# Second halves of the stacked keys, copied by transfers within SBUF

## The chip, the cores and the metric

The kernel runs on one core of one Trainium2 chip. The metric is the device time of one execution in microseconds (us). The core's engines work side by side, each down a list of its own in order: TensorE (PE, matrix products; its weight loads are listed as PEld), VectorE (DVE), ScalarE (ACT), GpSimd (POOL) and SyncE (SP), which here does nothing but issue transfers. An engine waits where an instruction needs a result of another one, and semaphores carry that.

## The reference, cut to what matters

One transformer block on a sequence of 512 rows of width 1024, in fp32: a modulation of `c` (`ada`), a layer norm, projections, two kinds of attention, an output projection, and a feed-forward part with a causal convolution.

```
mod = silu(c) @ w_ada + b_ada
u = layer_norm(x) * (1 + sc1) + sh1
qa, ka, va, qb, kc, vc, ksl, vsl, kw, vw, gl = split(u @ w_in)
o_a = dilated_attention(rope(qa), rope(ka), va)           # 8 heads of 64
o_b = nsa_attention(rope(qb), rope(kc), vc, rope(ksl), vsl, rope(kw), vw, gl, ...)
y = concat([o_a, o_b]) @ w_o
x = layer_norm(ALPHA * x + g1 * y, ln1_g, ln1_b)
u = layer_norm(x) * (1 + sc2) + sh2
a_gate, a_val = split(u @ w_up)
h = gelu(causal_dwconv(a_gate, conv_w, conv_b)) * a_val
x = layer_norm(ALPHA * x + g2 * (h @ w_down), ln2_g, ln2_b)
```

What the change touches are the scores, a query times the keys of a head (64 numbers each), for the dilated attention (`ka`) and for two of the three branches of the other (`ksl`, `kw`).

## The kernel before

Products are made at fp32 accuracy from fp32r operands: each operand is split into a high part (the value copied by ACT into fp32r, which rounds it) and a low part (the value less the high part, by DVE), and three products high x high, low x high and high x low are added up (`mm3`, the lines 259 to 261).

For scores this is done with a stack. A head has 64 rows, PE takes 128. `q_stack` puts the high part of a query in one half of the 128 partitions and its low part in the other half: `qe` for the head in the lower half, `qo` for the one in the upper half. `k_half` makes two tiles of 128 x 512 for a head: `hh` (named khh) with the key's high part in both halves, and `ll` (kll) with its low part in both halves. One product of the query stack with khh then gives high x high + low x high, and a second with kll adds the rest (lines 700 and 701). `e` says in which half of the transposed keys (`pt`, named qT) the head stands: `b` is its own half, `c0` the other one.

`k_half` runs 12 times: four times for the other attention's keys in the opening (`kb`, through `k_stack`, lines 1270 and 1273; khh_853/kll_854, 859/860, 910/911, 916/917) and twice for each of the four quads of dilated heads, a0 to a3 (line 955).

Time runs in stages. Up to about 55 us the modulation, the layer norm and the first products run; to 300 us the attention. There, PE's products of the remaining projections (`quad`, weights 512 KB each, loaded by SP into four buffers `wraw`, split by ACT and DVE into whi and wlo) fill the room between the rows of attention. A row of attention is a chain over the engines: scores on PE (L700, L701), mask and minimum on DVE (L708, `sa_`), exponential on ACT (L714), reciprocal on DVE (L719), scaling on POOL (L722), transposes on PE (L727), a split on ACT and DVE (L746, L750), products with the values on PE (L775). Compressed keys have a chain of their own (L645 to L675, with `pc` and `sm_`). Beside these stand the columns of the modulation (`ada_col`: a load and one DVE product with a sum, L1019) and its rows (`ada_row`, `arow`), and the two-layer compression (`hid`, with the weights k_w1 and v_w1). The output projection w_o, the up projection (325 to 540 us) and the down projection (to the end) follow.

All loads of weights go through `load` (L240) on SP's queue, one behind the other in the list: an entry that waits holds those behind it. Each transfer there also waits for the one eight places ahead of it in the list to have landed, as the kernel is built.

The order of the instructions on each engine is not that of the program text alone: the code interleaves generators (`fill_one`, `run_misc`), and the scheduler of the tile framework places each instruction by a simulated time at which its operands are ready. So a change in `k_half` also changes the order elsewhere.

Of the kernel before, what the change touches and what calls it, by code (L numbers as in the profile page):

```python
# [14 lines left out]
AF = mybir.ActivationFunctionType  # L15
# [91 lines left out]
def body(ctx, tc, nc, a, out, dbg=None):  # L107
# [59 lines left out]
    V, A, P, T = nc.vector, nc.scalar, nc.gpsimd, nc.tensor  # L167
# [68 lines left out]
    def f(x):  # L236
        return x.bitcast(F32)

    def load(dst, src, queue=nc.sync):
        queue.dma_start(dst, src)  # L240
# [230 lines left out]
        V.tensor_sub(o[0:64], pt[64:128], f(o[64:128]))  # L471
        return e, o

    def k_half(pt, e, mk=t2):
        b, c0 = 64 * e, 64 - 64 * e
        hh, ll = mk('khh'), mk('kll')
        A.activation(hh[b:b + 64], pt[b:b + 64], AF.Copy)
        A.activation(hh[c0:c0 + 64], pt[b:b + 64], AF.Copy)
        V.tensor_sub(ll[b:b + 64], pt[b:b + 64], f(hh[b:b + 64]))
        V.tensor_copy(ll[c0:c0 + 64], f(ll[b:b + 64]))  # L480
        return hh, ll

    def k_stack(pt, mk=t2):
        return [k_half(pt, e, mk) for e in range(2)]
# [446 lines left out]
    def a_post(j):  # L931
        mk = to if j == 0 else t2

        def run(banks):
            ys = []
            for b in range(2):
                yield from wk_wait(1)
                ys.append(evac_half(banks[b], b, 2, P))
                acc_done()
                yield 1 + b * PD  # L940
            yield from acc_wait()
            live[0] += 1
            pt = transposed(ys, 0, 'acc')
            yield 2
            qa[j] = q_stack(pt, mk)
            acc_done()
            yield 3
            yield from acc_wait()
            live[0] += 1
            pt = transposed(ys, 1, 'acc')  # L950
            wlive[0] -= 2
            yield 2
            ka[j] = []
            for b in range(2):
                ka[j].append(k_half(pt, b, mk))
                if b == 1:
                    acc_done()
                    ready.add(('a', j))
                yield
        return run  # L960
# [585 lines left out]
```

## Time and profile before

| | us |
|---|---|
| median of 3 runs | 726.68 |
| lowest and highest | 724.72, 728.5 |
| profiled execution | 726.39 |
| its span, from the first to the last instruction | 724.6 |

In the span, PE is busy 95%, DVE 64%, ACT 48%, POOL 34%. Busy time is a sum over stages of different kinds; what bounds a stage is read from the stretch itself: from the instruction before which PE stood idle, and from what released it. The granted clock of PE is given as a share of full speed, 1.00 being its upper level (2.4 GHz) and 0.50 its lower (1.2 GHz).

### The profile page before, as it was taken

The page shows a single profiled execution, that of the slowest core. Times are in us where ns is not written, and L with a number is a line of the kernel's source. Part 1 is how long each engine was busy: PE and PEld are TensorE (multiplying, and loading weights), DVE is VectorE, ACT ScalarE, POOL GpSimd, SP SyncE. Part 2 cuts the span into 40 slices and gives each one's busy share as a digit, 9 for nine tenths or more (in the row PEclk, how much of TensorE's full clock was granted, in tenths as well). Part 3 has the DMA queues.
Part 4 walks back from the last instruction along what each step waited for, and adds up shares of the span by engine and source line. Part 5 has one row for each costly group of instructions (what it writes and reads, how often), then busy time and mean ns, then how long its engine had stood idle before and what let it go on. Part 6 is the DMA issues. An engine that isn't in the chain of part 4 may idle for free.

```text
span 724.6 us, 10875 instructions
## 1 busy us (share of the span) xinstructions
PE 691.1 (95%) x3964; PEld 596.8 (82%) x3964; DVE 464.8 (64%) x961; ACT 345.7 (48%) x697; POOL 248.7 (34%) x273
## 2 busy tenths in 40 slices
PE   7999899999889998999999999999999999999995
PEld 6999788987879887778898888888888788888884
DVE  7879966766986889988843344464443364544236
ACT  5647665752767689916553333333333341222101
POOL 2002436441277475511310110111111355666216
PEclk9999999999999999999999999999999999999998
DMA  9955342046451011260112224434423233343002
GB/s 340 386 207 206 131 135 86 30 174 238 140 204 60 29 60 58 86 235 1 59 60 87 88 88 145 140 135 161 145 88 116 88 107 126 116 146 121 25 15 101
DMA packets 29149, 89.93 MB, mean 124 GB/s; under 512 B 3748, under 2 KB 4516, under 8 KB 29096
## 3 DMA queue, kind: packets, MB, share of 16 engines
q1 hardware_dynamic: 28660, 89.05, 35.6%
q8 instruction: 31, 0.51, 0.3%
q10 hardware_dynamic: 436, 0.18, 0.1%
q14 instruction: 22, 0.18, 0.1%
HBM read 87.13 MB, written 2.10 MB: 123 GB/s over the span
## 4 chain that ended last, share of the span: by engine, by line
PE 51%; DVE 3%; POOL 1%; issue 1%; ACT 0%; POOLq 0%; DVEq 0%
PE d L261 6%; PE d L260 6%; PE d L259 5%; PE pvv L259 5%; PE pvv L261 5%; PE pvv L260 5%; PE pg L259 5%; PE pg L261 5%; PE pg L260 5%; DVE x L1355 1%; PE wo L261 1%; PE wo L260 1%; PE wo L259 1%; DVE x L1346 0%; DVE bn L299 0%
## 5 line engine op out<-in xcount | busy, mean ns | idle before, releaser
L256 DVE TENSOR_TENSOR wlo<-wraw,whi 128x1024 fp32r<-128x1024 f32 x60 | 86.2, 1437 | 124.8 <-ACT whi L255 123.6
L255 ACT ACTIVATE whi<-wraw 128x1024 fp32r<-128x1024 f32 x60 | 63.6, 1060 | 142.9 <-PE pg L260 70.4
L259 PE MATMUL quad<-whi,u 128*128 128x256 f32 x256 | 75.0, 294 | 1.0 <-DVE qo L471 1.0
L260 PE MATMUL quad<-wlo,u 128*128 128x256 f32 x256 | 72.8, 284 | 0.0
L261 PE MATMUL quad<-whi,u 128*128 128x256 f32 x256 | 72.6, 284 | 0.0
L1498 POOL TENSOR_TENSOR wraw<-wraw,arow 128x1024 f32<-128x1024 f32 x22 | 57.8, 2633 | 35.3 <-DMA wraw<-w_down 28.6
L259 PE MATMUL pg<-u,whi 128*128 128x512 f32 (+1 forms) x176 | 67.7, 385 | 0.0
L260 PE MATMUL pg<-u,whi 128*128 128x512 f32 (+1 forms) x176 | 66.8, 380 | 0.0
L261 PE MATMUL pg<-u,wlo 128*128 128x512 f32 (+1 forms) x176 | 66.8, 379 | 0.0
L261 PE MATMUL pvv<-u,wlo 128*128 128x512 f32 (+1 forms) x176 | 66.8, 379 | 0.0
L259 PE MATMUL pvv<-u,whi 128*128 128x512 f32 (+1 forms) x176 | 66.8, 379 | 0.0
L260 PE MATMUL pvv<-u,whi 128*128 128x512 f32 (+1 forms) x176 | 66.8, 379 | 0.0
L256 POOL TENSOR_TENSOR hl<-cv,hh 128x512 fp32r<-128x512 f32 x14 | 23.9, 1705 | 110.8 <-ACT hh L255 110.8
L259 PEld LDWEIGHTS quad<-whi,u 128*128 128x128 f32 x256 | 48.7, 191 | 5.7 <-issue 3.9
L708 DVE CUSTOM_DVE_ANT_0 p<-sp,masks 128x128 f32<-128x128 f32 (+1 forms) x96 | 45.0, 482 | 8.8 <-PE sp L701 7.9
L260 PEld LDWEIGHTS quad<-wlo,u 128*128 128x128 f32 x256 | 48.9, 191 | 1.0 <-issue 0.4
L261 PEld LDWEIGHTS quad<-whi,u 128*128 128x128 f32 x256 | 48.9, 191 | 0.1
L727 PE MATMUL pT<-ident,p 128*128 128x128 f32 x240 | 39.8, 280 | 4.6 <-POOL p L722 4.2
L260 PEld LDWEIGHTS pg<-u,whi 128*128 128x128 f32 x176 | 33.1, 188 | 6.6 <-issue 0.5
L256 POOL TENSOR_TENSOR hg<-cv,hg 128x512 fp32r<-128x512 f32 x8 | 12.9, 1609 | 74.9 <-ACT hg L255 74.9
L259 PEld LDWEIGHTS pg<-u,whi 128*128 128x128 f32 x176 | 33.1, 188 | 6.6 <-issue 0.5
L261 PEld LDWEIGHTS pvv<-u,wlo 128*128 128x128 f32 x176 | 33.1, 188 | 6.3
(636 smaller groups left out, 1884.7 us busy)
## 6 DMA issues: line engine op xcount, KB each, us to landing
wraw<-w_up SPq DMA_DIRECT2D x44, 512.0 KB, 3.2
wraw<-w_down SPq DMA_DIRECT2D x22, 512.0 KB, 3.4
ada<-ada_col SPq DMA_DIRECT2D x32, 256.0 KB, 6.0
wraw<-w_quad SPq DMA_DIRECT2D x16, 512.0 KB, 4.9
wraw<-ada_col SPq DMA_DIRECT2D x16, 512.0 KB, 3.3
wraw<-ada_row SPq DMA_DIRECT2D x16, 512.0 KB, 3.6
x<-x SPq DMA_DIRECT2D x8, 512.0 KB, 4.8
wraw<-w_o SPq DMA_DIRECT2D x8, 512.0 KB, 3.2
```

Of the source, the lines that this page charges most:

```text
L255: A.activation(hi, raw, AF.Copy)
L256: lo_engine.tensor_sub(lo, raw, f(hi))
L259: T.matmul(o_, sh, mh, start=start, stop=False)
L260: T.matmul(o_, sh, ml, start=False, stop=False)
L261: T.matmul(o_, sl, mh, start=False, stop=stop)
L708: V.tensor_tensor_reduce(p[:, cols[i]], e['s'][:, cols[i]], masks[:, m0:mask0 + 512], 1.0, 3e38, op0=ALU.add, op1=ALU.min, accum_out=m_[:, ...
L727: T.transpose(e['t'][:, 128 * j:128 * j + 128], e['p'][:, 128 * j:128 * j + 128], ident)
L1355: V.scalar_tensor_tensor(src[:, hs], src[:, hs], ag[:, 3:4], b_[h][:, cs], op0=ALU.mult, op1=ALU.add)
L1498: P.tensor_mul(w, w, g2)
```

## The change

In `k_half` the second copy of the high part (an ACT copy into the other half) and of the low part (a DVE copy into the other half) are replaced by two transfers from SBUF to SBUF of 64 x 512 fp32 (128 KB), on SP's queue. A new argument `spare` is true by default, and no call sets it, so all 12 calls take the new way; the four lines of the old way stay in the text behind it, unused.

```diff
-    def k_half(pt, e, mk=t2):
+    def k_half(pt, e, mk=t2, spare=True):
         b, c0 = 64 * e, 64 - 64 * e
+        if spare:
+            hh, ll = mk('khh'), mk('kll')
+            A.activation(hh[b:b + 64], pt[b:b + 64], AF.Copy)
+            load(f(hh[c0:c0 + 64]), f(hh[b:b + 64]))
+            V.tensor_sub(ll[b:b + 64], pt[b:b + 64], f(hh[b:b + 64]))
+            load(f(ll[c0:c0 + 64]), f(ll[b:b + 64]))
+            return hh, ll
         hh, ll = mk('khh'), mk('kll')
         A.activation(hh[b:b + 64], pt[b:b + 64], AF.Copy)
         A.activation(hh[c0:c0 + 64], pt[b:b + 64], AF.Copy)
```

Line numbers behind this place rise by 7: the mask step of the softmax is L708 before and L715 now.

The order of DVE in the opening, before. `kll_911` and `kll_917` are the low parts of the second pair of keys, `qe_927` and `qo_928` the second query stack, `wraw_1002` a column load of the modulation, `p_981` the first row's softmax.

```order
L479 TENSOR_TENSOR kll_911<-qT_905,khh_910 64x512
L1019 ISA wraw_1002,mod_164<-wraw_1002,crow_86,b_col_78 128x1024
L1019 ISA mod_164 128x1
L480 CAST kll_911<-kll_911 64x512
L479 TENSOR_TENSOR kll_917<-qT_905,khh_916 64x512
L708 ISA p_981,sa__982<-sp_969,masks_709 128x128
L708 ISA sa__982 128x1
L480 CAST kll_917<-kll_917 64x512
L708 ISA p_981,sa__982<-sp_969,masks_709 128x256
L708 ISA sa__982 128x1
L470 TENSOR_TENSOR qe_927<-qT_922,qe_927 64x512
L471 TENSOR_TENSOR qo_928<-qT_922,qo_928 64x512
```

And the same place now:

```order
L480 TENSOR_TENSOR kll_911<-qT_905,khh_910 64x512
L1026 ISA wraw_975,mod_164<-wraw_975,crow_86,b_col_78 128x1024
L1026 ISA mod_164 128x1
L480 TENSOR_TENSOR kll_917<-qT_905,khh_916 64x512
L470 TENSOR_TENSOR qe_927<-qT_922,qe_927 64x512
L471 TENSOR_TENSOR qo_928<-qT_922,qo_928 64x512
L715 ISA p_981,sa__982<-sp_969,masks_709 128x128
L715 ISA sa__982 128x1
L715 ISA p_981,sa__982<-sp_969,masks_709 128x256
L715 ISA sa__982 128x1
```

The two copies are gone, the query stack comes ahead of the softmax, and the product with the column load stands here with `wraw_975`, which before stood ahead of the first query stack; the one with `wraw_1002` is now 12 rows behind this piece, after two more softmax steps. On PE the score products of the second and third group stand 13 and 12 places further ahead than before; the first product of a1's first row with kll stands 18 places further back.

The order of SP at the same time, as a piece of the difference (a row with + is new):

```order
 L240 DMA wraw_975<-ada_col 128x1024
+L240 DMA khh_853<-khh_853 64x512
+L240 DMA kll_854<-kll_854 64x512
+L240 DMA khh_859<-khh_859 64x512
+L240 DMA kll_860<-kll_860 64x512
+L240 DMA khh_910<-khh_910 64x512
 L240 DMA wraw_989<-w_quad 128x1024
+L240 DMA kll_911<-kll_911 64x512
+L240 DMA khh_916<-khh_916 64x512
+L240 DMA kll_917<-kll_917 64x512
 L240 DMA wraw_1002<-ada_col 128x1024
 L240 DMA wraw_1030<-ada_col 128x1024
```

The eight transfers of the opening stand between four weight loads; the load of k_w1 follows the last row shown.

The order of DVE at a2 (about 250 us), before. `pc` and `sm_` belong to two rows of the compressed keys' chain, `pcl` to the row ahead of them.

```order
L479 TENSOR_TENSOR kll_3233<-qT_3215,khh_3232 64x512
L646 TENSOR_TENSOR pc_3266<-pc_3266,sc_3206 128x256
L480 CAST kll_3233<-kll_3233 64x512
L647 TENSOR_REDUCE sm__3265<-pc_3266 128x8
L655 TENSOR_REDUCE sm__3221<-pc_3222 128x8
L479 TENSOR_TENSOR kll_3250<-qT_3215,khh_3249 64x512
L648 TENSOR_TENSOR pc_3266<-pc_3266,sm__3265 128x256
L480 CAST kll_3250<-kll_3250 64x512
L656 RECIPROCAL sm__3221<-sm__3221 128x8
L675 TENSOR_TENSOR pcl_3057<-pcT_3255,pch_3055 128x128
L657 SCALAR_TENSOR_TENSOR sm__3221<-sm__3221,cvalid_713,gates_717 128x8
```

And now:

```order
L480 TENSOR_TENSOR kll_3233<-qT_3215,khh_3232 64x512
L653 TENSOR_TENSOR pc_3266<-pc_3266,sc_3206 128x256
L662 TENSOR_REDUCE sm__3221<-pc_3222 128x8
L480 TENSOR_TENSOR kll_3250<-qT_3215,khh_3249 64x512
L654 TENSOR_REDUCE sm__3265<-pc_3266 128x8
L663 RECIPROCAL sm__3221<-sm__3221 128x8
L655 TENSOR_TENSOR pc_3266<-pc_3266,sm__3265 128x256
L664 SCALAR_TENSOR_TENSOR sm__3221<-sm__3221,cvalid_713,gates_717 128x8
```

Between the first low part and the last step on `sm__3221` there stand six instructions instead of nine.

## Rows read from the trace of the kernel before

**Rows 1.** The page's first part: busy time of an engine, its share of the span, and its instructions.

```profile
PE 691.1 (95%) x3964; PEld 596.8 (82%) x3964; DVE 464.8 (64%) x961; ACT 345.7 (48%) x697; POOL 248.7 (34%) x273
```

**Rows 2.** Busy time by stage: the stretch, its length, busy us (and instructions) of PE, PEld, DVE, ACT and POOL, then the granted clock, the share of the DMA engines and GB/s.

```profile
60.00:90.00 30.00, 26.67 (x189) 23.93 (x189) 28.30 (x73) 19.23 (x43) 12.79 (x15) 0.94 0.52 178
...
240.00:280.00 40.00, 35.33 (x266) 31.92 (x265) 36.61 (x104) 30.17 (x81) 23.65 (x35) 1.00 0.20 67
280.00:300.00 20.00, 19.21 (x123) 16.04 (x123) 19.57 (x63) 18.96 (x52) 9.89 (x16) 1.00 0.00 1
325.00:540.00 215.00, 213.55 (x1047) 180.56 (x1047) 114.34 (x169) 92.33 (x158) 35.52 (x33) 1.00 0.30 101
```

**Rows 3.** The timeline of PE in the opening, the score products before which it stood idle, and the first product of `hid`: start, duration, line, operation; in brackets the idle time before and what ended it.

```profile
71.34 0.30 PE L700 MATMUL sp<-khh,qe 128*128 128x128 f32 x1 [1.11 <-DVE qo L471]
...
76.17 0.45 PE L700 MATMUL sp<-khh,qe 128*128 128x384 f32 x1 [1.27 <-DVE sa__982 L708]
...
77.59 0.50 PE L700 MATMUL sp<-khh,qe 128*128 128x512 f32 x1 [0.68 <-DVE qo L471]
...
78.59 0.48 PE L700 MATMUL sp<-khh,qe 128*128 128x128 f32 x1 [0.26 <-DVE sa__1023 L708]
...
85.05 0.86 PE L1146 MATMUL hid<-wraw,bst 128*62 128x256 f32 x3
```

**Rows 4.** DVE in the opening: first the group of the four copies of low parts in 60 to 90 us (busy us, mean ns, then idle before), then rows of the timeline, with columns as in rows 3.

```profile
L480 DVE CAST kll<-kll 64x512 fp32r<-64x512 f32 x4 | 2.8, 688 | 0.1
...
64.72 0.68 DVE L479 TENSOR_TENSOR kll<-qT,khh 64x512 fp32r<-64x512 f32 x1
...
66.84 1.28 DVE L1019 CUSTOM_DVE_ANT_0 wraw<-wraw,crow,b_col 128x1024 f32<-128x1024 f32 x1 [0.40 <-DMA wraw<-ada_col]
...
70.50 0.69 DVE L471 TENSOR_TENSOR qo<-qT,qo 64x512 fp32r<-64x512 f32 x1
...
73.03 0.08 DVE L1019 DVE_READ_ACCUMULATOR2_ANT mod<- 128x1 f32 x1
...
76.03 0.08 DVE L708 DVE_READ_ACCUMULATOR2_ANT sa__982<- 128x1 f32 x1
...
76.84 0.69 DVE L471 TENSOR_TENSOR qo<-qT,qo 64x512 fp32r<-64x512 f32 x1
```

**Rows 5.** Short stretches of the opening, of a1's place and of a2's, with columns as in rows 2.

```profile
70.00:75.00 5.00, 3.79 (x30) 3.41 (x29) 4.86 (x9) 3.84 (x7) 4.71 (x6) 1.00 0.37 129
75.00:78.40 3.40, 1.47 (x5) 0.77 (x5) 3.28 (x10) 1.79 (x7) 0.38 (x1) 1.00 0.20 76
78.40:81.80 3.40, 3.21 (x14) 3.22 (x15) 3.40 (x15) 1.79 (x7) 2.58 (x3) 0.50 0.00 0
...
181.00:184.20 3.20, 1.36 (x14) 1.12 (x12) 3.14 (x8) 3.16 (x7) 0.00 (x0) 1.00 0.39 151
184.20:187.70 3.50, 3.50 (x17) 2.98 (x15) 3.41 (x8) 2.05 (x5) 2.55 (x4) 0.51 0.34 117
...
250.00:255.00 5.00, 3.19 (x25) 2.78 (x24) 4.80 (x17) 3.10 (x9) 0.61 (x1) 1.00 0.00 0
```

**Rows 6.** The groups of the second copies in 60 to 310 us: busy us, mean ns, idle before them.

```profile
L478 ACT ACTIVATE khh<-qT 64x512 fp32r<-64x512 f32 x12 | 7.1, 592 | 0.1
...
L480 DVE CAST kll<-kll 64x512 fp32r<-64x512 f32 x12 | 6.1, 511 | 0.4
```

**Rows 7.** SP's queue in the opening: the issue of the first k_w load (start, duration of the issue).

```profile
73.14 0.33 SPq L240 DMA_DIRECT2D wraw<-k_w  x1
```

**Rows 8.** The DMA issues of the whole span: what is written from what, the queue, how many, KB each, and the median us from issue to landing.

```profile
wraw<-w_quad SPq DMA_DIRECT2D x16, 512.0 KB, 4.9
wraw<-ada_col SPq DMA_DIRECT2D x16, 512.0 KB, 3.3
...
o<-x SPq DMA_DIRECT2D x7, 256.0 KB, 2.0
...
ident<-ident ACTq DMA_DIRECT2D x1, 64.0 KB, 5.6
...
cmask<-cmask SPq DMA_DIRECT2D x1, 64.0 KB, 5.0
```

**Rows 9.** The places of a0 and a1: rows of PE's and DVE's timeline, and the stretch 140 to 145 us with columns as in rows 2.

```profile
144.07 0.22 PE L700 MATMUL sp<-khh,qe 128*128 128x128 f32 x1
...
142.01 0.68 DVE L479 TENSOR_TENSOR kll<-qT,khh 64x512 fp32r<-64x512 f32 x1 [1.23 <-PE pvb L775]
...
140.00:145.00 5.00, 4.88 (x41) 4.76 (x41) 3.62 (x8) 4.09 (x8) 0.66 (x1) 1.00 0.02 3
...
186.79 0.68 DVE L479 TENSOR_TENSOR kll<-qT,khh 64x512 fp32r<-64x512 f32 x1
...
189.88 0.22 PE L701 MATMUL sp<-kll,qe 128*128 128x128 f32 x1
...
183.73 0.67 PE L462 MATMUL qT<-ident,yq 128*128 128x128 f32 x4 [1.84 <-ACT arow L1031]
```

**Rows 10.** The place of a2: the last small step on DVE, the product on POOL and the transposes on PE that follow it, and the first score product of this stack.

```profile
253.82 0.22 DVE L657 SCALAR_TENSOR_TENSOR sm__3221<-sm__3221,cvalid,gates 128x8 f32<-128x8 f32 x1
...
254.21 0.61 POOL L660 TENSOR_TENSOR pc<-pc,sm__3221 128x256 f32<-128x256 f32 x1 [7.39 <-DVE sm__3221 L657]
...
254.88 0.44 PE L665 MATMUL pcT<-ident,pc 128*128 128x128 f32 x2 [1.52 <-POOL pc L660]
...
277.94 0.30 PE L700 MATMUL sp<-khh,qe 128*128 128x128 f32 x1
```

## The prediction

> **What bounds the kernel now.** I read the page's head first, then a table of short stretches, then the idle gaps in front of single instructions. The head shows TensorE (PE) busy 691.1 us of 724.6 [rows 1], so the kernel is PE's list of products, and a change to other engines gains only where PE stands idle or runs at a lower clock. The table by stage shows where it does not: 213.55 of 215.00 us busy in 325 to 540 [rows 2]. There nothing can be won, but time won ahead of this stretch is carried through it, since it starts earlier.
>
> The key stacks are built at five places: twice two in the opening (62 to 77 us) and for a0, a1, a2, a3. In the opening PE stands before four score products, 1.11 + 1.27 + 0.68 + 0.26 = 3.3 us, each time for VectorE (DVE) [rows 3]: for the query stack (qo, L471) or for the first softmax step (sa__982). DVE's gaps there are small; it works down a list on which the key copies (L480) stand ahead of what PE waits for [rows 4]. The stretch behind this shows a second price: PE was busy 1.47 of 3.40 us in 75.0 to 78.4, and in the next 3.4 us, busy 3.21, the granted clock was 0.50, the lower of its two levels (1.2 GHz) [rows 5]. The same pair stands at 181.0 (1.36 of 3.20, then 0.51); after 3.19 of 5.00 in 250 to 255 I saw no such fall [rows 5].
>
> **The change part by part.** It removes 12 ScalarE (ACT) copies of 592 ns (7.1 us) and 12 DVE copies of 511 ns (6.1 us) [rows 6], and adds 24 transfers of 128 KB on SP's queue. In program order every one of them is issued behind its ACT or DVE result, and loads behind it wait too.
>
> Opening, DVE. The four copies cost 2.8 us here [rows 4]. By the order, L471 of the first stack now also stands ahead of one ada_col product (1.28 us and 0.4 us of waiting for its load), which before stood in front of it. It ended at 71.19; less two copies at the mean of 0.69 and 1.7 this gives 68.1. The first copy's operand, kll, is ready at 65.4 at the latest (64.72 + 0.68) [rows 4]; with DVE's earlier rows unchanged but for one ada_col product behind it rather than ahead, about 64.1. PE came to its first score at 71.34 - 1.11 = 70.2 [rows 3], so the copy has 4.8 to 6 us. The second L471 ended at 77.53; less four copies (2.8), one product (1.28, moved behind the softmax steps), 0.4, and the two softmax steps that now follow it (0.9), it ends at 72.2, and the softmax that PE waited for at 73.1 instead of 76.11. By the order PE meets the second and third group of scores twelve or thirteen places sooner in its list, so a rest of its waits can stay; I keep 0.6 of the 3.3 us and take 2.7 (bounds 1 and 3.3).
>
> Opening, clock. If PE does not run dry, the stretch at 0.50 goes. Its 3.21 us of work take half: 1.6 us. I take it whole, since the stretch ahead of it would then be nearer to 3.19 of 5.00 than to 1.47 of 3.40. The bounds are 0 and 1.6. Together 4.3: DVE's softmax steps come 3 us sooner, and the rest hangs on the clock.
>
> Opening, queue. The last kll copy waits for a DVE result at about 71, and three loads behind it (two of ada_col, and k_w) are held until then. The two ada_col products are behind the softmax steps on DVE's list, which covers this. The k_w load was issued at 73.14, as the ada_col product that ended at 73.11 freed its buffer [rows 4, 7]. That product now ends near 77; the load, at the 3.3 us of ada_col loads of its size [rows 8], lands at 80.3. PE came to it at 85.05 [rows 3], and now at 85.05 - 4.3 = 80.75. So it is just in time: 0 to 1 us lost, I take 0.2. ACT's four copies count for nothing, since it was idle a third of this stage (19.23 of 30.00 busy) [rows 2].
>
> How long a copy takes no row shows, since before has no transfer from SBUF to SBUF. The nearest row by size, queue and idle DMA engines is that of the outputs, 2.0 us for 256 KB; the longest of small ones are loads at the start, 5.0 (cmask, 64 KB) and 5.6 (ident, 64 KB) [rows 8]. I take 2.3, nearer to the first, as the DMA engines are 2% busy at a0 [rows 9]; I keep 2.0 and 5.6 for the range.
>
> The Trainium skill, "DMA: Bandwidth & Descriptors", section "Anatomy of one DMA — SWDGE (gpsimd) path", states about 2.0 us fixed plus the bytes at 436 GB/s; by that an estimate for 128 KB is 2.3 us. It states this for another path than SP's, and no run here shows it; by it the sum would be the same.
>
> a0. DVE's kll ends at 142.69 [rows 9], after 1.23 us of waiting for PE, and perhaps 0.6 sooner now; PE takes the first score at 144.07 without waiting. Copy ready at 142.1 + 2.3 = 144.4: 0.3 us lost (0 at 2.0, 3.6 at 5.6).
>
> a1. kll ends at 187.47, and the copy makes it ready at 189.8. Before, PE used it at 189.88 [rows 9]; by the order this product now stands 18 places later in PE's list, at about 191. An ada_col load in front of the copy, issued as DVE begins L479 at 186.79, would land by the same 3.3 us at 190.1. Lost: 0 (2.1 at 5.6).
>
> a2. DVE's run of small steps ends with L657 at 254.04; GpSimd (POOL) has stood 7.39 us for it, and PE 1.52 us for POOL's product [rows 10]. Two copies (0.84 us) leave this run, and by the order this step (L664 now) no longer stands behind a pcl product, 0.2 or 0.3 more. Gained: 1.1 (0.8 to 1.5). The scores of this stack come over 20 us later, from 277.94 [rows 10], which covers its copies; at SP two loads of w_o wait behind them that are issued long after.
>
> a3. DVE is busy 36.61 of 40.00 and 19.57 of 20.00 us around it, PE 35.33 and 19.21 [rows 2]; two DVE copies (0.84) and two of ACT (1.18) leave. PE is short of both by turns, so I take half of DVE's part, 0.4 (0 to 0.8).
>
> Sum: -(2.7 + 1.6) + 0.2 + 0.3 + 0 - 1.1 - 0.4 = -5.3. The profiled execution took 726.39 us (its span 724.6 and 1.8 around it), which is 0.3 under the median of 726.68. So 721.1 beside that execution and 721.4 beside the median.
>
> **Rivals.**
> First, only part arrives. PE's list between 70 and 85 also waits for exponentials on ACT and scaling on POOL, which the copies don't touch; then the dip shrinks but the clock still falls (1.6 not won), and a third of the waits stays (1.0), with a3 at 0. For: ahead of the other fall PE stood 1.84 us for ACT [rows 9]. Against: all four gaps of the opening name DVE. -5.3 + 1.6 + 1.0 + 0.4 = -2.3: 724.4.
>
> Second, slower: the copies land late, and PE waits for them in place of DVE. With L us from the issue to the use, the loss is L - 2.0 at a0 (142.1 against 144.07), L - 3.5 at a1 (187.47 against 191), and L - 5 in the opening (the second pair's kll, ready near 69, used near 74). Against it stands what the rest wins, 4.3 + 1.1 + 0.4 - 0.2 = 5.6. Break-even is 3L - 10.5 = 5.6, L = 5.4, between the cmask and the ident row; with L = 7.5 it is 12.0 - 5.6 = +6.4: 733.1. For: in the opening the copies are queued behind 512 KB loads of which w_quad's take 4.9 us [rows 8]. Against: at a0 and a1, where the most would be lost, the queue has little ahead of it, and the output rows are at 2.0.
>
> The rule in the same section of the Trainium skill that a semaphore wait is made on the issuing sequencer, before dispatch, speaks against the change: what stands behind a waiting copy is held. The order of SP has this form, and no run here shows its price yet.
>
> Third, nothing comes of it: the time is set by loads or by later stages that give all back, as each stretch with a free buffer waits for SP. PE loses 4.7 us of 40 in 240 to 280 [rows 2], a stretch that may lose more when it is reached sooner. 726.7.
>
> **How the numbers follow.** A measurement of this kernel can tell about 0.5% from no change, here 723.0 and 730.3. Forecast 0.50 (716.5 to 723.5, of which 0.47 is under 723.0); part arrives 0.27 (722 to 726.5, 0.08 under 723.0); late copies 0.13 (726 to 738, 0.08 above 730.3); nothing 0.10. Faster 0.56 (with 0.01 from the last), same 0.35, slower 0.09. The range 717.0 to 727.5 leaves out the far end of the first case and most of the late copies.
>
> **What would show it.** Right: L479's successors on DVE close up, no idle before the scores at 70 to 79, PEclk 1.00 there, copies landing in 2 to 3 us, and pcT without its 1.52 us. Wrong: idle before score products that ends with a DMA of khh or kll (second rival); half clock still after 75 (first); the hid product waiting for k_w by over 1 us (queue). A profile with the opening 4 us shorter and the end unchanged is the third rival.

## The result and the profile after

The changed kernel takes 722.43 us (median of 7 runs, 720.7 to 726.81), the kernel before 726.58 (7 runs, 724.62 to 728.5). The ratio is 0.9947, with a 95% interval of 0.9928 to 0.9966: faster by 0.5%. In a second set, beside other kernels, it was 0.9944 (0.9922 to 0.9966). The profiled execution is the fastest of the seven (720.7, span 718.9); it stands 5.7 us under the profiled one of before, while the medians are 4.15 apart. Part of this scatter goes with the granted clock: the three runs with a mean clock of 0.986 took 723.31, 724.6 and 726.81, the four between 0.988 and 0.993 took 720.7 to 722.43. It isn't all of it: in the second set the two runs with 0.987 were the fastest of seven (721.13 and 721.8, the others at 0.990).

The opening first. The timeline of PE, as in [rows 3]: score products, the idle time ahead of them, and the first product of `hid`.

```profile
69.61 0.22 PE L707 MATMUL sp<-khh,qe 128*128 128x128 f32 x1
...
71.92 0.44 PE L707 MATMUL sp<-khh,qe 128*128 128x384 f32 x1 [0.37 <-DVE qo L471]
...
79.86 0.50 PE L707 MATMUL sp<-khh,qe 128*128 128x512 f32 x1 [0.73 <-DVE sa__1095 L715]
...
80.87 1.05 PE L1153 MATMUL hid<-wraw,bst 128*62 128x256 f32 x4
```

Of the 3.3 us ahead of scores 1.1 are left, and `hid` starts at 80.87 instead of 85.05. Of these 4.2 us, 0.44 were there already at 55 us (the last `comp` product starts at 55.18 instead of 55.62), so the opening itself gives 3.7. The stretches, as in [rows 5]:

```profile
65.00:70.00 5.00, 5.00 (x44) 4.82 (x43) 4.86 (x8) 3.65 (x7) 2.89 (x3) 1.00 1.00 247
70.00:75.00 5.00, 4.63 (x35) 4.30 (x35) 4.78 (x18) 4.26 (x13) 4.60 (x8) 1.00 0.89 264
75.00:78.40 3.40, 3.40 (x31) 3.40 (x30) 2.25 (x6) 1.68 (x7) 1.04 (x2) 1.00 0.23 94
78.40:81.80 3.40, 2.61 (x15) 1.65 (x13) 3.40 (x11) 2.07 (x6) 1.03 (x1) 1.00 0.81 289
```

PE is busy all of 75.0 to 78.4 (1.47 of 3.40 before), and the clock stays at 1.00 where it had been 0.50. The DMA share, the last column but one, is higher: 1.00 in 65 to 70 and 0.89 behind it, where it was 0.77 and 0.37. DVE shows what that means (columns as in [rows 4]):

```profile
67.11 0.69 DVE L471 TENSOR_TENSOR qo<-qT,qo 64x512 fp32r<-64x512 f32 x1
...
71.17 0.69 DVE L471 TENSOR_TENSOR qo<-qT,qo 64x512 fp32r<-64x512 f32 x1
...
76.15 1.28 DVE L1026 CUSTOM_DVE_ANT_0 wraw<-wraw,crow,b_col 128x1024 f32<-128x1024 f32 x1 [1.27 <-DMA wraw<-ada_col]
```

The first qo ends at 67.80 instead of 71.19, the second at 71.86 instead of 77.53. Then DVE stands 1.27 us for an ada_col load. SP's queue says why, and when k_w goes out:

```profile
70.47 0.79 SPq L240 DMA_DIRECT2D kll<-kll  x1
71.31 1.23 SPq L240 DMA_DIRECT2D wraw<-ada_col  x2
77.47 0.33 SPq L240 DMA_DIRECT2D wraw<-k_w  x1
```

The two ada_col loads, issued at 66.0 to 68.5 before, go out from 71.3 on, behind the last kll copy. The DMA issues, as in [rows 8], of the new transfers:

```profile
khh<-khh SPq DMA_DIRECT2D x12, 128.0 KB, 2.3
kll<-kll SPq DMA_DIRECT2D x12, 128.0 KB, 3.0
```

Further on, a0's score waits 0.56 us for a copy, and the wait of a2's pcT, 1.52 us in [rows 10], is 0.26:

```profile
142.48 0.30 PE L708 MATMUL sp<-kll,qe 128*128 128x128 f32 x1 [0.56 <-DMA kll<-kll]
...
248.30 0.44 PE L672 MATMUL pcT<-ident,pc 128*128 128x128 f32 x2 [0.26 <-POOL pc L667]
```

From here to the end the lead stays: the first product of w_o starts 5.94 us sooner, the last product of the down projection 5.67.

### The profile page after: what moved, and what is told of

It reads as the page before. It is cut to its first block, busy times and chain, and to the rows that moved or that the text cites. A ratio compares the mean times of both kernels' runs of the same rounds, so it can differ in the third digit from the quotient of the medians.

```text
span 718.9 us, 10914 instructions
## 1 busy us (share of the span) xinstructions
PE 690.4 (96%) x3964; PEld 597.2 (83%) x3964; DVE 457.6 (64%) x949; ACT 338.6 (47%) x685; POOL 251.5 (35%) x273
## 4 chain that ended last, share of the span: by engine, by line
PE 77%; DVE 10%; ACT 4%; POOL 4%; issue 3%; DMA 2%; POOLq 0%; SPq 0%; DVEq 0%; ACTq 0%
PE d L259 6%; PE d L261 6%; PE d L260 6%; PE pvv L260 5%; PE pvv L259 5%; PE pvv L261 5%; PE pg L260 5%; PE pg L259 5%; PE pg L261 5%; PE first L393 3%; PE quad L259 3%; PE quad L260 3%; PE quad L261 3%; PE pT L734 2%; PE hid L1153 2%
## 5 line engine op out<-in xcount | busy, mean ns | idle before, releaser
L256 DVE TENSOR_TENSOR wlo<-wraw,whi 128x1024 fp32r<-128x1024 f32 x60 | 80.3, 1339 | 122.7 <-ACT whi L255 121.6
L1505 POOL TENSOR_TENSOR wraw<-wraw,arow 128x1024 f32<-128x1024 f32 x22 | 59.3, 2707 | 33.9 <-DMA wraw<-w_down 27.1
L715 DVE CUSTOM_DVE_ANT_0 p<-sp,masks 128x128 f32<-128x128 f32 (+1 forms) x96 | 44.7, 483 | 11.5 <-PE sp L708 11.3
L259 PEld LDWEIGHTS pvv<-u,whi 128*128 128x128 f32 x176 | 33.1, 188 | 6.3
```

Of the source, the lines that this page charges most:

```text
L256: lo_engine.tensor_sub(lo, raw, f(hi))
L259: T.matmul(o_, sh, mh, start=start, stop=False)
L715: V.tensor_tensor_reduce(p[:, cols[i]], e['s'][:, cols[i]], masks[:, m0:mask0 + 512], 1.0, 3e38, op0=ALU.add, op1=ALU.min, accum_out=m_[:, ...
L1505: P.tensor_mul(w, w, g2)
```

## The experiments

My theory: the gain is made in the opening, where PE waits for DVE's list, plus about 1 us at a2, less a loss at a0; the loads held on SP and the late landings are a price that is covered. The rivals: the gain sits in the dilated stacks, or in the clock, or in the new order alone; or the transfers cost and a version without their cost would be faster. The edits are given against the changed kernel.

**Which place.** `opening_only` gives the transfers to `kb` alone, `dilated_only` to a0 to a3 alone; the other calls use the four lines of before.

```diff
-        return [k_half(pt, e, mk) for e in range(2)]
+        return [k_half(pt, e, mk, True, True) for e in range(2)]
...
-    def k_half(pt, e, mk=t2, spare=True):
+    def k_half(pt, e, mk=t2, hi=False, lo=False):
```

(for `dilated_only` True and False the other way round)

> Only the eight second copies of the opening are made by transfers; a0 to a3 keep their ACT and DVE copies. If the gain comes from the opening, as the trace of the changed kernel reads (first hid product 4.2 us earlier, 0.4 of it already there at 60 us), this run keeps 3.7 to 4.3 us of it: 722.2 to 723.2, hid near 81, no half clock in 78 to 82, and no PE wait for a kll transfer at a0. If the gain is spread over the dilated stacks, or is chance in the granted clock, it stays at 724.5 to 726.5.

> Only the sixteen second copies of a0 to a3 are made by transfers; the opening keeps its ACT and DVE copies. By my sum: a0 loses 0.3 to 0.7, a2 wins 1.1 to 1.5, a3 0.4, so 725.0 to 726.0, with the opening's waits of 3.3 us and its half clock unchanged. If the dilated stacks carry the gain, 722.5 to 724.0. If late landings are the price that the opening hides, above 726.6.

Measured: `opening_only` 723.51, ratio 0.9963 (0.9944 to 0.9982); `dilated_only` 725.06, ratio 0.9985 (0.9970 to 1.0000). The two gains add to 0.52%, the whole change has 0.53 and 0.56. So the medians bear out the shares of the theory, seven tenths of the gain in the opening, though the interval of `dilated_only` reaches no change at all; `opening_only` is a little over the range that I gave it. In `opening_only` the first hid product comes at 80.55 and the clock of the opening stays whole; in `dilated_only` the opening is that of before, with the same pair of stretches:

```profile
75.00:78.40 3.40, 1.65 (x7) 0.95 (x7) 3.31 (x12) 1.88 (x8) 0.02 (x1) 1.00 0.11 45
78.40:81.80 3.40, 3.40 (x16) 3.40 (x17) 3.13 (x13) 1.91 (x6) 2.59 (x3) 0.50 0.02 6
```

The two also tell the landing apart. First `opening_only`, then `dilated_only`:

```profile
khh<-khh SPq DMA_DIRECT2D x4, 128.0 KB, 4.5
kll<-kll SPq DMA_DIRECT2D x4, 128.0 KB, 4.7
```

```profile
khh<-khh SPq DMA_DIRECT2D x8, 128.0 KB, 2.2
kll<-kll SPq DMA_DIRECT2D x8, 128.0 KB, 2.4
```

A copy lands in 2.2 to 2.4 us where the queue is quiet, and in 4.5 to 4.7 in the opening.

**Which engine.** `low_only` sends only the low parts by transfer (ACT keeps its copies), `high_only` only the high parts (DVE keeps its copies), at all twelve places.

```diff
-            load(f(hh[c0:c0 + 64]), f(hh[b:b + 64]))
+            A.activation(hh[c0:c0 + 64], pt[b:b + 64], AF.Copy)
```

(`low_only`; in `high_only` the other `load` is replaced by DVE's copy)

> Only the low parts (DVE's copies) go by transfer, at all twelve places; ACT keeps its copies of the high parts. If DVE's list is the bound, most of the gain is here: 722.8 to 724.3, with the first hid product at 81.5 to 83. If ACT's copies matter as much, 724.5 to 725.5.

> Only the high parts (ACT's copies) go by transfer, at all twelve places; DVE keeps its copies of the low parts. ACT had room (19.23 of 30 us busy in the opening), so 725.3 to 727.0 if DVE's list is the bound, with idle of PE before the first scores as before. If ACT's copies matter as much, 723.5 to 725.0.

Measured: `low_only` 727.74, ratio 1.0021 (1.0008 to 1.0035), slower than before; `high_only` 725.04, ratio 0.9990 (0.9973 to 1.0007), no change that can be told. Neither half brings the gain, and the theory that DVE's copies alone are the bound falls. The trace of `low_only`, DVE and PE:

```profile
69.68 0.69 DVE L471 TENSOR_TENSOR qo<-qT,qo 64x512 fp32r<-64x512 f32 x1
...
72.99 1.68 DVE L1025 CUSTOM_DVE_ANT_0 wraw<-wraw,crow,b_col 128x1024 f32<-128x1024 f32 x1 [1.90 <-DMA wraw<-ada_col]
...
78.01 0.69 DVE L471 TENSOR_TENSOR qo<-qT,qo 64x512 fp32r<-64x512 f32 x1
```

```profile
71.49 0.33 PE L707 MATMUL sp<-kll,qe 128*128 128x128 f32 x1 [0.67 <-DMA kll<-kll]
...
76.13 0.44 PE L706 MATMUL sp<-khh,qe 128*128 128x384 f32 x1 [1.76 <-DVE sa__982 L714]
...
78.76 0.79 PE L706 MATMUL sp<-khh,qe 128*128 128x512 f32 x1 [1.29 <-DVE qo L471]
```

With ACT's copies in place the scheduler leaves the ada_col product of wraw_1002 ahead of the softmax on DVE, and puts one more (1.28 us) ahead of the second qo. The load of wraw_1002 isn't held here:

```profile
66.20 0.53 SPq L240 DMA_DIRECT2D wraw<-ada_col  x1
```

Before, it was issued at 66.02 and landed in 4.9 us. Here it lands just before its product starts at 72.99, more than 6.5 us after its issue, while the DMA engines' share in 70 to 75 is 0.69 (0.37 before), and DVE stands 1.90 us for it. This and the added product eat what the copies gave, and PE waits for sa__982 and qo as before. In the changed kernel the same load is issued even later, at 71.31, but its product stands behind two more softmax steps, and DVE's 1.27 us of waiting cost PE 0.73 at one score. `high_only` shows the other half: the ada_col product is out of the way, but DVE's four copies are not, and PE stands 1.95 us for sa__982:

```profile
73.25 0.44 PE L706 MATMUL sp<-khh,qe 128*128 128x384 f32 x1 [1.95 <-DVE sa__982 L714]
```

**The order without the time, as intended.** `kept_opening` makes the transfers in the opening and both engines' copies too, into a tile that nobody reads.

```diff
+            xh = to('xkh')
...
+            A.activation(xh[c0:c0 + 64], pt[b:b + 64], AF.Copy)
...
+            V.tensor_copy(xh[b:b + 64], f(ll[b:b + 64]))
```

(in the opening; a0 to a3 as before the change)

> In the opening only, the transfers are made, and ACT and DVE make their second copies too, into a tile that nobody reads; a0 to a3 as before the change. The scheduler then puts the ada_col product behind the softmax, as in the changed kernel, while the work on DVE stays. If the freed engine time is what counts, PE keeps most of its 3.3 us of waiting for qo and sa__982 and the half clock after it, and the time is 725.5 to 727.5. If the order is what counts (that product out of the way), at least half of the opening's gain is here: 723.5 to 725.

Measured: 727.09, ratio 1.0019 (1.0002 to 1.0036). The ada_col product of wraw_1002 stands behind the softmax, and yet nothing is won: PE is at its first score at 71.61 with 2.22 us of idle, as the first qo ends at 71.50 (71.19 before).

```profile
71.61 0.30 PE L709 MATMUL sp<-khh,qe 128*128 128x128 f32 x1 [2.22 <-issue]
```

But the order of the changed kernel did not come about. The product of wraw_975 stands ahead of the first qo, as before the change, and waits for its load, and three softmax steps stand ahead of the second qo, which ends at 77.90 (DVE):

```profile
66.77 1.67 DVE L1028 CUSTOM_DVE_ANT_0 wraw<-wraw,crow,b_col 128x1024 f32<-128x1024 f32 x1 [1.26 <-DMA wraw<-ada_col]
...
70.81 0.69 DVE L471 TENSOR_TENSOR qo<-qT,qo 64x512 fp32r<-64x512 f32 x1
```

So this run doesn't show what the order alone is worth. What all the traces show is what goes with ACT's copies: where they are made in the opening (before, `dilated_only`, `low_only`, `kept_opening`), four ada_col products, counted from the start, stand ahead of the first qo, and it ends at 70.37 to 71.50; in the ten other profiles three do, and it ends at 67.80 to 68.92. By the times alone both kinds of copies must go: neither half gave the gain. How much of it is freed time and how much is order stays open.

**What the landing and the hold cost.** `twice` makes every transfer twice, the second behind the first.

```diff
             load(f(hh[c0:c0 + 64]), f(hh[b:b + 64]))
+            load(f(hh[c0:c0 + 64]), f(hh[b:b + 64]))
...
             load(f(ll[c0:c0 + 64]), f(ll[b:b + 64]))
+            load(f(ll[c0:c0 + 64]), f(ll[b:b + 64]))
```

> Each of the 24 transfers is made twice, the second behind the first, so that a copy lands about twice as late and SP holds the loads behind it longer. If the landing is what PE and the loads see at a0 and in the opening, PE's wait for kll at a0 grows from 0.56 to about 2.5 us or more, the first k_w load is issued 1 to 2 us later than the 77.5 of the changed kernel and hid waits for it; 725.5 to 728.5. If the transfers are covered everywhere (they cost nothing beyond what the trace shows), 722 to 723.5.

Measured: 725.21, ratio 0.9987 (0.9973 to 1.0001): some 3 us of the gain are gone. In PE's waits the price stands at the weight loads, more than at the copies: four loads, the first k_w load among them, go out only from 77.97 to 79.61, right behind the last copy. PE's rows:

```profile
71.36 0.30 PE L708 MATMUL sp<-khh,qe 128*128 128x128 f32 x1 [0.98 <-DMA khh<-khh]
...
86.42 1.94 PE L1154 MATMUL hid<-wraw,bst 128*62 128x256 f32 x8 [0.47 <-DMA wraw<-k_w]
...
94.08 1.94 PE L1154 MATMUL hid<-wraw,bst 128*62 128x256 f32 x8 [2.00 <-DMA wraw<-k_w]
```

PE waits 2.47 us for the k_w loads and 1.0 for the first copies. The 2.5 us that I expected at a0 did not show, since the scheduler set a0's first score further back.

**Without any transfer in the opening.** `zero_opening` leaves the second halves there uncopied: GpSimd sets them to zero.

```diff
-            load(f(hh[c0:c0 + 64]), f(hh[b:b + 64]))
+            P.memset(f(hh[c0:c0 + 64]), 0.0)
...
-            load(f(ll[c0:c0 + 64]), f(ll[b:b + 64]))
+            P.memset(f(ll[c0:c0 + 64]), 0.0)
```

> In the opening the second halves are not copied at all; GpSimd sets them to zero ahead of time, so the scores of these heads leave out part of their three products. a0 to a3 as in the changed kernel. This shows what the freed ACT and DVE time is worth without any transfer. If the eight transfers cost by holding loads and by filling the DMA engines, hid comes 0.5 to 2 us before the changed kernel's 80.9 and the time is 720 to 721.5, 1 to 2 us under after_again. If they are covered, it is within 0.5 us of after_again.

> The changed kernel once more, beside the other three. 721.5 to 723.5, with the opening as in its first profile: no half clock between 70 and 90 us in the profiled execution and hid near 81.

Measured: `zero_opening` 723.47, ratio 0.9950 (0.9932 to 0.9969); `after_again` 722.54, ratio 0.9944. No transfer, and no gain over the changed kernel. The trace shows another order: with no copies on SP the scheduler puts one more ada_col product ahead of the second qo (as in `pool_both` below), DVE waits for its load and PE for DVE, and the half clock is back (DVE, PE, and the stretch):

```profile
71.96 1.32 DVE L1033 CUSTOM_DVE_ANT_0 wraw<-wraw,crow,b_col 128x1024 f32<-128x1024 f32 x1 [1.24 <-DMA wraw<-ada_col]
...
74.77 0.69 PE L714 MATMUL sp<-khh,qe 128*128 128x384 f32 x1 [2.20 <-DVE qo L471]
...
75.00:78.40 3.40, 3.40 (x15) 3.20 (x16) 2.92 (x15) 2.48 (x9) 1.56 (x4) 0.55 0.29 116
```

So this run does not price the transfers by themselves: no transfers with one more product ahead of qo, and eight transfers without it, can't be told apart by the time. In `after_again` the opening is as in the first profile, a little less good: 1.08 us for qo and 0.65 for sa__1095, hid at 82.01, no half clock between 65 and 86.

**Other ways for the copies.** Four versions tried to keep the gain and drop the hold. `opening_act_high` issues the opening's high parts on ACT's queue:

```diff
-            load(f(hh[c0:c0 + 64]), f(hh[b:b + 64]))
+            load(f(hh[c0:c0 + 64]), f(hh[b:b + 64]), A)
```

(in the opening). `act_high_a0` is this, with a0's low parts copied by DVE.

> As the changed kernel, but in the opening the high parts' transfers are issued on ACT's queue, and the low parts' ones stay on SP, where the load of wraw_1002 (ada_col) now stands between them. If the hold on SP costs, DVE's 1.27 us of waiting for that load at 76 goes, the first k_w load is issued about 1.3 us sooner, PE's 0.7 us at 79.9 shrink, and the time is 720.8 to 722.0. If the hold is covered, 722 to 723; if the issues on ACT cost as much as the copies did, 723.5 or more.

> As opening_act_high, and the two low parts of a0 are copied by DVE again. PE's 0.56 us of waiting for the kll transfer at a0 goes and 0.84 us of DVE work comes back where DVE waits for PE anyway: 0.3 to 0.6 us under opening_act_high, 720.3 to 721.6. If DVE's list is the bound there too, no gain or up to 0.4 us more than opening_act_high.

Measured: 723.99, ratio 0.9972 (0.9957 to 0.9987), and 723.80, ratio 0.9974 (0.9962 to 0.9987). Both medians are a little above the changed kernel's, with intervals that overlap with its own. In `opening_act_high` the load of wraw_1002 is issued at 67.58 instead of 71.31, but DVE gets it at 77.49, after 2.63 us of waiting, and the second pair's copies come late to PE:

```profile
76.16 0.30 PE L706 MATMUL sp<-khh,qe 128*128 128x128 f32 x1 [1.00 <-DMA khh<-khh]
...
77.91 0.47 PE L707 MATMUL sp<-kll,qe 128*128 128x128 f32 x1 [1.45 <-DMA kll<-kll]
```

The earlier issue did not help while the DMA engines were full (a share of 1.08 in 74 to 76 here): what waited on SP before its issue now waits behind it, 9.9 us from its issue to the end of DVE's wait. Nor is ACT freed: its four issues take 0.47 to 0.52 us each, little less than the 592 ns of a copy in [rows 6]. What a0's copy by DVE gives back does not show: 0.2 us is inside the noise.

`pool_high` lets GpSimd copy the opening's high parts, `pool_both` both parts.

```diff
-            load(f(hh[c0:c0 + 64]), f(hh[b:b + 64]))
+            P.tensor_copy(hh[c0:c0 + 64], f(hh[b:b + 64]))
```

> In the opening the high parts are copied by GpSimd and the low parts by transfer on SP; a0 to a3 as in the changed kernel. Half the bytes leave the DMA engines and wraw_1002's load stands ahead of two of the copies. If DMA load and hold are the price, DVE's 1.27 us of waiting for that load shrinks and the time is 720.5 to 722. If GpSimd's copies delay its scaling of the first rows, 723 to 725.

> In the opening GpSimd makes both second copies, no transfer there; a0 to a3 as in the changed kernel. GpSimd was idle until 67 us and then busy to 75 with the sums for hid. If it has room, 720 to 722; if its eight copies push the sums and the scaling of the first rows back, PE waits for p and for kll and it is 723.5 to 727.

Measured: 723.96, ratio 0.9976 (0.9958 to 0.9994), and 725.88, ratio 0.9992 (0.9972 to 1.0011). GpSimd has no room: its sums for hid end later, so does the scaling of the first rows, and PE waits for p, twice 1.2 us in `pool_high` and 2.66 in `pool_both`. First `pool_high`, then `pool_both`:

```profile
76.44 0.33 PE L741 MATMUL pT<-ident,p 128*128 128x128 f32 x1 [1.18 <-POOL p L736]
78.00 0.44 PE L741 MATMUL pT<-ident,p 128*128 128x128 f32 x2 [1.23 <-POOL p L736]
```

```profile
79.82 1.23 PE L741 MATMUL pT<-ident,p 128*128 128x128 f32 x3 [2.66 <-POOL p L736]
```

No version tried has a lower median than the changed kernel; the intervals of `opening_only`, `zero_opening`, `opening_act_high`, `act_high_a0` and `pool_high` overlap with its own.

## Why the prediction was right, and where it was not

The forecast was 721.4, the median is 722.43: faster, as forecast, by 4.2 instead of 5.3 us. Step by step:

- **Opening, DVE: 2.7 us of PE's waits go.** 2.2 went in the first profile (3.3 to 1.1) and 1.6 in the second. The ends of the two qo were to be 68.1 and 72.2 and are 67.80 and 71.86. What was mis-sized is the rest: the wait for sa__1095 (0.73) is new; two ada_col products, the first of them late by its held load, stand ahead of the end of that softmax step.
- **Opening, clock: 1.6 us.** Right for this place, in both profiles and in `opening_only`. In most versions in which PE ran dry there (before, `low_only`, `high_only`, `dilated_only`, `zero_opening`) the fall stayed, but not in all: in `pool_high` PE is busy 0.99 of 3.40 us, less than before the change, and the clock stays at 1.00.

```profile
75.00:78.40 3.40, 0.99 (x8) 0.60 (x7) 3.40 (x15) 0.00 (x0) 3.29 (x4) 1.00 0.48 154
78.40:81.80 3.40, 3.40 (x29) 3.36 (x28) 1.91 (x8) 2.58 (x8) 1.23 (x2) 1.00 0.45 154
```

So that the dip decides whether the clock falls, as this step has it, is not borne out, and the step came right without its reason being shown. It also left out that a fall can come elsewhere (below).
- **Opening, queue: k_w issued near 77, hid near 80.75 and just in time.** Issued at 77.47, hid at 80.87, without a wait for k_w.
- **"ACT's four copies count for nothing".** This step failed. `low_only` takes only DVE's copies away and is slower than before by 0.2%. Only with ACT's copies gone do the two ada_col products leave the way of qo and the softmax (the product of wraw_975 with its wait is the 1.7 us in the working of the first qo's end). My sum used the new order as a given and put its worth down to DVE's copies.
- **A copy lands in 2.3 us.** Right where the DMA engines are idle (2.2 and 2.4), wrong by a factor of two in the opening (4.5 and 4.7). It cost PE no wait there, but only just: the first kll copy, issued at 63.63, took 5.7 us to land, and PE used it at 69.67; I had worked out a cover of 4.8 to 6 us. The estimate of 2.3 us from the figures of the Trainium skill's "DMA: Bandwidth & Descriptors", section "Anatomy of one DMA — SWDGE (gpsimd) path", which are stated for another path, agrees with the quiet places and not with the opening.
- **a0: 0.3 us lost.** 0.56. **a1: 0.** No wait for a copy there.
- **a2: 1.1 us won.** The wait fell from 1.52 to 0.26 (0.25 in `dilated_only`, 1.53 in `opening_only`).
- **a3: 0.4 us won.** Not found. Between the last pcT and the first w_o product the lead shrinks from 6.63 to 5.94 us, and in `dilated_only` from 2.78 to 2.06. No wait takes it: PE stands idle 2.08 us of this stretch before and now, and is busy 0.69 us longer, so a longer piece of its list stands between the two. First before, then after:

```profile
256.93:281.30 24.37, 22.29 (x158) 19.01 (x156) 22.16 (x63) 21.89 (x58) 17.29 (x25) 1.00 0.26 87
```

```profile
250.30:275.36 25.06, 22.98 (x159) 19.40 (x158) 22.97 (x64) 21.64 (x59) 17.47 (x26) 1.00 0.28 91
```

That the sum came near is in part luck. Compare the start of the same products in the two profiles: the changed kernel is ahead by 4.1 us at 123.56, by 2.6 at 137.55, by 4.1 at 179.61, by 5.2 at 244.37, by 6.6 behind a2's pcT and by 5.9 at w_o. The 1.6 us lost behind 123 are the new fall of the clock (below). The 1.5 us won next lie at a0 and a1, where the sum had a loss of 0.3: a wait of 1.06 us before a hid product is gone, and that of 1.84 us before a1's transposes ([rows 9]) is 0.94. First before, then after:

```profile
146.11 1.91 PE L1146 MATMUL hid<-wraw,bst 128*62 128x256 f32 x8 [1.06 <-issue]
```

```profile
142.99 1.94 PE L1153 MATMUL hid<-wraw,bst 128*62 128x256 f32 x8
...
179.61 0.66 PE L462 MATMUL qT<-ident,yq 128*128 128x128 f32 x4 [0.94 <-ACT arow L1038]
```

The wait of 1.06 is gone in `dilated_only` too and stays in `opening_only`, so it goes with the dilated stacks; what PE stood for there the profile does not show. The two errors, a loss and a gain, nearly cancel.

Of the rivals, the late copies fell: even with every copy made twice, in `twice`, the kernel was not shown to be slower than before, and the larger part of PE's waits stood at hid. That only part arrives is not far off: a third of the waits stays, as it said (half in the second profile), while the clock's fall was moved and not kept. That a transfer which waits holds what is behind it is seen in the trace: the ada_col loads go out from 71.31 on instead of 66.0 to 68.5. It goes with 1.27 us of DVE's waiting in the changed kernel, and in `twice` with 2.47 us of PE's at hid. The Trainium skill's "DMA: Bandwidth & Descriptors" states in the same section that a semaphore wait is made on the issuing sequencer, before dispatch; the trace agrees.

What stays open: how much the eight transfers cost by themselves at the same order, and how much the new order gives by itself, since every edit of the copies also moved ada_col products or softmax steps.

## What to carry to other kernels

Where a scheduler orders the work, an edit's worth lies in what the new order lets pass as much as in the engine time that it frees: neither half of this change gave the gain, the two together did, and each had to be read from the order and the trace together. A copy put on the queue of the weights is cheap only as long as the loads behind it are not the next thing waited for, so look up, for each held load, who uses it and when.

## What was not expected of the hardware

For each byte the copies within SBUF took more of the DMA engines than the loads. In the changed kernel 138.8 to 144.4 us holds only a0's four copies, 144.4 to 150 only loads:

```profile
138.80:144.40 5.60, 5.04 (x36) 4.18 (x36) 5.20 (x12) 4.51 (x12) 1.03 (x2) 1.00 0.44 97
144.40:150.00 5.60, 5.60 (x44) 5.13 (x43) 2.39 (x7) 2.19 (x8) 0.82 (x2) 1.00 0.51 187
```

0.44 of the engines for 97 GB/s against 0.51 for 187: 1.7 times the share for a byte. By these two figures, an estimate, the opening's eight copies of 128 KB fill all the engines for 4.8 us, where loads of the same bytes would for 2.9. Where more is in flight the ratio is smaller: in `opening_act_high`, 58 to 84 us, the copies on ACT's queue (0.52 MB) have 8.2% of the engines' time, SP's queue (5.21 MB, mostly loads) 70.9%, 1.2 times for a byte. The copies have rows of 2 KB and the loads rows of 4 KB, and no run separates that from the source.

The clock's falls do not follow the size of the dip alone. Before, PE is busy 3.21 of 5.00 us in 125 to 130, and the clock stays; in the changed kernel the same dip, 3.23 of 5.00, comes 5 us sooner and the clock falls behind it. First before, then after:

```profile
125.00:130.00 5.00, 3.21 (x27) 3.01 (x26) 4.18 (x14) 3.96 (x12) 3.11 (x8) 1.00 0.00 0
130.00:135.00 5.00, 5.00 (x43) 4.91 (x42) 3.63 (x11) 4.09 (x11) 3.98 (x8) 1.00 0.00 0
```

```profile
120.00:125.00 5.00, 3.23 (x27) 3.02 (x27) 4.66 (x14) 3.40 (x10) 3.68 (x8) 1.00 0.00 0
125.00:130.00 5.00, 5.00 (x29) 4.81 (x29) 2.15 (x8) 2.96 (x10) 1.81 (x5) 0.66 0.00 2
```

PE works 5.00 us at 0.66 here, by an estimate 1.7 us lost, about what was won in the opening; on the other side the fall behind a1 in [rows 5] is gone. With `pool_high` above, where a deeper dip had no fall behind it, the runs do not show what decides this.
